# Transposes by pairs, spread tap tables, later stages and another slab order in a twelve-layer kernel

## The chip, the core and the metric

The kernel runs on one core of a Trainium2 chip. The core has a tensor engine (PE; its weight loads are listed apart as PEld), a vector engine (DVE), a scalar engine (ACT), GpSimd (POOL) and a queue engine (SP), which here only issues DMAs. The metric is the device time of one launch in microseconds, median of several runs, lower is better. A trace of one profiled execution tells where it went.

## What is computed

Fourteen sublayers act in turn on a residual x of 256 rows and 1024 columns in float32: a first block of four pairs (mixer, feed-forward) and a second block of two triples (feed-forward, mix, feed-forward). Each normalises x, multiplies it by weights that are read once from DRAM, and adds the result to x:

```python
def swiglu(h, w_gate_up, w_down):
    gate, up = jnp.split(h @ w_gate_up, 2, axis=-1)
    return (jax.nn.silu(gate) * up) @ w_down
...
def first_block(...):
    for i in range(DEPTH):               # 4: fourier, s5, attention, fourier
        h = rms_norm(x, norm_mix_g[i])
        ...
        x = x + mix.astype(x.dtype)
        h = rms_norm(x, norm_ffn_g[i])
        x = x + swiglu(h, ffn_w_gate_up[i], ffn_w_down[i]).astype(x.dtype)
```

The S5 mixer is, for 64 groups of 16 columns, a linear recurrence over the 256 positions in both directions, then a gate. The kernel cuts the positions into 32 chunks of 8: inside a chunk it convolves with tap tables, between chunks it scans. The dilated attention has three groups of 16 heads, whose results are weighted by the softmax of their log sums. A mix sublayer joins a state-space branch (decays from running sums of a step size over positions, 16 heads) and an attention branch over 64 keys chosen by an index score.

## The kernel before

**Weights.** All matrices come as 774 slabs of 128x1024 (512 KB), in the order in which they are used (the class W; `add_in` and `add_out` build the list, lines 246 to 255). SP loads a slab into one of four `raw` buffers (L156); ACT rounds it to `whi` (L168), DVE makes the rest `wlo` (L169). Every float32 product is three PE passes (L306, L307, L308: whi with hi, wlo with hi, whi with lo of the other side). A slab is 12 matmuls of 128x512.

**Order.** The program is written out in one go; each engine executes its own list in order. `slab_step` calls `S.tick()` twice in a slab, after six matmuls each. All other work is a task: `S.defer(fn, n)` puts it n ticks later, `S.pace(fns, every, wait)` puts several in a row, and `S.require(task)` forces a task, with those due earlier, where its result is needed. So the place of a transpose or a small product among the weight products is set by numbers of ticks.

**PSUM.** Four banks (`acc`) hold the sums of weight products, four (`aux`) everything else.

**Feed-forward** (`ffn`, eight of them). `in_proj` takes 11 blocks of four slabs. Each block's gate and up are evicted to `hb` (L467, L468); three ticks later a task of its own makes four transposes into one aux bank (L475) and `hT.put` splits them (L450, L451). `out_proj` takes 22 slabs: half 0, then half 1 of the 1024 output columns. At the end of a half x is updated (L433), and `half_ready` transposes it for the next layer (L380).

**S5.** Its tables are made during the first feed-forward by tasks on all engines, and kept in DRAM: wb (`s_wb`), ct (`s_ct`), and taps (`s_k`, written by POOL at L1572). In the S5 layer SP loads, in this order, wb, the four `local` tables (L1579: each 1 MB in eight pieces, 16 partitions of 16 runs of 128 numbers) and eight ct tables (L1541). PE makes the chunk ends (L1680, L817), then `part(k, 0)` for eight k with the local tables, and `part(k, 1)`, `part(k, 2)` with ct and the states H (L1758). DVE runs two scans, each of 30 steps of three operations (L1726, L1727, L1730): after the first ISC = 28 operations of scan 0 the two are interleaved, and ACT copies the states to H (L1740, L1741). While scan 1 goes on alone, DVE transposes the finished results (L1819). A task `rest` makes the last parts, k from 4 to 7, once scan 1 has ended.

**Attention.** `permuted_rstd` turns rsq of x to another order of rows by small products (L572), ahead of all blocks; it is needed from the second group of heads on. Then 18 blocks of four slabs make q, k and v; qk is evicted at L651 after transposes of qsq (L640). The heads are done in four units, each with four items (two head pairs by two row halves). `start_unit` runs the items as a pipeline, one item each AE = 4 ticks, with these stages and their ticks: scores 0 (PE L677), highest 1, exps 2, divide 4 (DVE, then POOL L696 on two tiles), probs 6 (PE L703), evict_probs 7 (ACT L711), values 10 (PE L723), put 11 (ACT L730, DVE L731). `oT.tasks` make the output product wait for put.

**Mix.** The first part of the state-space branch is paced on DVE and ACT, one step each SS = 3 ticks after STEPS = 6: decay, ratio, series, softplus, sums, keep, turn, spread. `spread` copies the running sums to `csT` (L1064), writes them to DRAM (L1066) and reads them back on all partitions as `csb` (L1069). Each head then needs ACT `seg` from csb (L1105), DVE (L1111), and PE (L1118 to L1120). The heads' place among the ticks is set by other joins, not by csb.

Of the kernel before, what the change touches and what calls it, by code (L numbers as in the profile page):

```python
# [17 lines left out]
P = 128  # L18
# [17 lines left out]
BB = 12  # L36
AR = 13
GD = 3
SS = 3
ISC = 28  # L40


DS = (0, 1, 2, 3, 4, 4, 5, 5)
# [11 lines left out]
ISM = 1000  # L55
EA = 11
UNITS = (None, 0, 1, 2, None, 3)
MIX_ORDER = tuple("qi bc x0 z0 x1 z1 q0 k0 v0 q1 k1 v1".split())


# [146 lines left out]
def tile_two_blocks(ctx: ExitStack, tc: tile.TileContext, A, out, upto=None, taps=None):  # L207
# [41 lines left out]
        for b, s in order_in(nblk):  # L249
            W.add(ap[base + b, s])  # L250

    def add_out(ap, nk):
        for h in range(2):
            for s in range(nk // 2):
                W.add(ap[h, s])

    layers = []
    for i in (range(6) if upto is None else upto):
        if i >= 4:
            i -= 4  # L260
            layers.append(("ffn1", i))
            add_in(A["ffn1_in"][i], 11)
            add_out(A["ffn1_out"][i], 22)
            layers.append(("mix", i))
            for b, s in order_in(12)[:8]:
                W.add(A["mix_in"][i, b, s])
            W.add(A["mix_small"][i])
            for b, s in order_in(12)[8:]:
                W.add(A["mix_in"][i, b, s])
            add_out(A["mix_out"][i], 16)  # L270
            layers.append(("ffn2", i))
            add_in(A["ffn2_in"][i], 11)
            add_out(A["ffn2_out"][i], 22)
            continue
        kind = i % 3
        if kind == 0:
            layers.append(("fourier", i))
            W.add(A["dft_d"])
            W.add(A["dft_t"])
            add_out(A["fnet_w_out"][i // 3], 8)  # L280
        elif kind == 2:
            layers.append(("attention", i))
            add_in(A["qkv"], 18)
            add_out(A["attn_o"], 8)
        else:
            layers.append(("s5", i))
            add_in(A["s5_glu"], 4)
        layers.append(("ffn", i))
        add_in(A["ffn_in"][i], 11)
        add_out(A["ffn_out"][i], 22)  # L290
# [131 lines left out]
                if b == 1 and after_head is not None:  # L422
                    after_head()

    def out_proj(src, nk, scale, xn):

        for h in range(2):
            ps = [acc() for _ in range(NT)]
            for s in range(nk // 2):
                slab_step(ps, src, 2 * s, W.take(), s == 0, s == nk // 2 - 1)  # L430
            for t in range(NT):
                xs = x[:, t, h * 512:(h + 1) * 512]
                nc.vector.scalar_tensor_tensor(xs, ps[t], scale, xs, OP.mult, OP.add)  # L433
            xn.half_ready(h)

    class Chunks:

# [20 lines left out]

    def ffn(xn, scale, nxt):
        hT = Chunks(22)  # L460

        def evict(b, ps):
            hb = tmp(name="hb")
            for t in range(NT):
# [2 lines left out]
                nc.scalar.activation(s, ps[t][:, :256], AF.Silu, scale=r)  # L467
                nc.vector.scalar_tensor_tensor(hb[:, t * 256:(t + 1) * 256], ps[t][:, 256:], r, s,  # L468
                                               OP.mult, OP.mult)

            def trans():
                pt = aux()
                for u in range(2):
                    for t in range(NT):
                        nc.tensor.transpose(pt[:, u * T + t * P:u * T + (t + 1) * P],  # L475
                                            hb[:, t * 256 + u * P:t * 256 + (u + 1) * P], ident)
                hT.put(2 * b, 2, pt)

            hT.tasks[2 * b] = hT.tasks[2 * b + 1] = S.defer(trans, 3)

        in_proj(xn, 11, evict)
        out_proj(hT, 22, scale, nxt)
# [73 lines left out]
    def attention(xn, nxt):  # L556
# [38 lines left out]
        def evict(b, ps):  # L595
            half, u, g = unit_block(b)
            if u is None:
                v = v_tile(half, g)
                for t in range(NT):
                    r = xn.rstd[:, t:t + 1] if g == 0 else rk[:, t:t + 1]  # L600
                    nc.scalar.activation(v[:, t], ps[t], AF.Copy, scale=r)
                if g == 2 and b // 3 % 3:
                    start_unit(UNITS[b // 3 - 1], 2)
                return
# [131 lines left out]

        def start_unit(u, wait):
            items = [(u, hp, t) for hp in range(2) for t in range(NT)]
            stages = ((put, 11), (values, 10), (evict_probs, 7), (probs, 6), (divide, 4), (exps, 2),
                      (highest, 1), (scores, 0))  # L740

            def step(n):
# [14 lines left out]
            return xn.chunk if u is not None or g == 0 else xn.chunk_by_parity  # L757

        S.require(xn.tasks[0])
        permuted_rstd()  # L760
        in_proj(xn, 18, evict, src)
        out_proj(oT, 8, 1.0, nxt)

    TWO_PI = (6.28125, 0.0019350051879882812, 2 * math.pi - 6.28125 - 0.0019350051879882812)
    ROUND = 1.5 * 2 ** 23
# [54 lines left out]
    def mixer(xn, nxt, li):  # L820
# [193 lines left out]
        def steps():  # L1014
# [55 lines left out]
                                                             ap=[[0, P], [1, 8 * T]]))  # L1070
                bc_ready()

            S.pace([decay, ratio, lambda: series((15, 13, 11, 9)), softplus, sums, keep, turn, spread], SS, STEPS)

        def similar():

# [199 lines left out]
    class S5:  # L1276
# [5 lines left out]
        def __init__(self):  # L1282
# [6 lines left out]
            self.wb_d = dram.tile([8, P, 2048], F32, name="s5_wb")  # L1289
            self.ct_d = dram.tile([8, P, 2048], F32, name="s5_ct")  # L1290
            self.kd = dram.tile([16, P, 240], F32, name="s5_k")
            self.wb, self.ct = {}, {}
            self.plan()

# [248 lines left out]
        def taps(self, m, ct):  # L1543
# [27 lines left out]
            if m % 2 == 1:  # L1571
                nc.gpsimd.dma_start(self.kd[m - 1:m + 1, :112].rearrange("m k x -> k m x"),  # L1572
                                    self.kt[:112, :480].rearrange("p (m x) -> p m x", m=2))

        def load_local(self, i):
            t = big(F32, "local")
            kd = self.kd.rearrange("m (q k) x -> k (m q) x", q=4)
            for j in range(8):
                nc.sync.dma_start(t[16 * j:16 * j + 16].rearrange("p (g x) -> p g x", g=16),  # L1579
                                  kd[:16, 16 * i:16 * i + 16, (7 - j) * 16:(7 - j) * 16 + 128])  # L1580
            return t

        def first_half(self, xn):
# [460 lines left out]
```

## Time and profile before

| | |
|---|---|
| time, median of 3 runs | 2555.62 us (2554.61 to 2557.14) |
| time of the profiled execution | 2555.06 us |
| its span | 2553.1 us |
| PE busy | 2460.1 us, 96% |
| DVE busy | 1615.5 us, 63% |
| ACT busy | 1331.1 us, 52% |
| POOL busy | 106.8 us, 4% |
| DRAM read, written | 437.57 MB, 16.50 MB |

Times in the trace count from the start of the span. The stretches that matter: the first feed-forward from 65 to 288.6 us, S5 from there to about 372, attention from 593.4 to 917.3, the two mix layers from 1523.4 to 1753.7 and from 2127.1 to 2357.4. In a timeline a row is a start, a duration, the engine, the line, the operation, and in brackets the idle time ahead of it with what ended it; rows of the same kind that follow each other are joined, with their count. Durations of matmuls overlap, so the cost of one is the distance of starts. A granted clock (PEclk) of 1.00 is 2.4 GHz, 0.50 is 1.2 GHz.

### The profile page before, as it was taken

The numbers are of one execution on the slowest core, as the hardware profiler recorded it, in microseconds if no ns is written. First come the engines' busy times: TensorE is split into PE (matmuls) and PEld (weight loads), VectorE is DVE, ScalarE is ACT, GpSimd is POOL, SyncE is SP. The second block draws the span as 40 slices with busy tenths as digits, with TensorE's granted clock in tenths as the row PEclk, the third lists the DMA queues.
The fourth block names the chain that finished last, engine by engine and source line by source line (L and its number), as shares of the span: only waits on it lengthen the run. The fifth ranks groups of instructions, "written<-read, shape, count | busy, mean of one in ns | idle before, by whom it ended". The sixth has DMA issues, their size and how long they took to land.

```text
span 2553.1 us, 34833 instructions
## 1 busy us (share of the span) xinstructions
PE 2460.1 (96%) x13048; PEld 2021.0 (79%) x13048; DVE 1615.5 (63%) x2847; ACT 1331.1 (52%) x2029; POOL 106.8 (4%) x127
## 2 busy tenths in 40 slices
PE   8999869999999999999999999999999999999998
PEld 7788558887777778888888888788888888788886
DVE  7988766554665655556555557776555555876554
ACT  5445555444555554444444446675444445775543
POOL 0111000000131410000000000000000000000000
PEclk9999979999999999999999999999999999999999
DMA  5777785665544546545555554545555555535554
GB/s 181 233 234 240 206 225 178 189 191 168 171 132 160 153 141 190 180 129 189 190 185 187 182 188 155 182 121 185 183 190 180 190 180 179 185 118 166 186 183 145
DMA packets 131850, 456.35 MB, mean 179 GB/s; under 512 B 14794, under 2 KB 23893, under 8 KB 129249
## 3 DMA queue, kind: packets, MB, share of 16 engines
q1 hardware_dynamic: 123616, 426.96, 52.8%
q0 software_dynamic: 7488, 26.51, 3.3%
q8 instruction: 103, 1.69, 0.3%
q10 hardware_dynamic: 576, 0.66, 0.1%
q14 instruction: 67, 0.54, 0.1%
HBM read 437.57 MB, written 16.50 MB: 178 GB/s over the span
## 4 chain that ended last, share of the span: by engine, by line
PE 41%; issue 29%; DVE 3%; ACT 2%; POOL 1%; DMA 1%; POOLq 0%; ACTq 0%; DVEq 0%
PE acc L306 12%; PE acc L308 12%; PE acc L307 12%; DVE wlo L169 1%; POOL sc L696 1%; PE aux L817 1%; ACT whi L168 1%; PE aux L475 1%; DMA csb<-cs_d 1%; PE aux L640 0%; PE aux L677 0%; PE aux L1213 0%; PE aux L703 0%; PE aux L723 0%; PE aux L380 0%
## 5 line engine op out<-in xcount | busy, mean ns | idle before, releaser
L169 DVE TENSOR_TENSOR wlo<-raw,whi 128x1024 fp32r<-128x1024 f32 (+1 forms) x774 | 922.2, 1219 | 371.7 <-ACT whi L168 370.0
L168 ACT ACTIVATE whi<-raw 128x1024 fp32r<-128x1024 f32 (+1 forms) x774 | 788.9, 1054 | 266.4 <-PE acc L308 245.3
L306 PE MATMUL acc<-whi,xhi 128*128 128x512 f32 (+1 forms) x2104 | 844.3, 401 | 2.1 <-DVE yflo L505 2.1
L307 PE MATMUL acc<-wlo,xhi 128*128 128x512 f32 (+1 forms) x2104 | 822.2, 391 | 3.2 <-DVE wlo L169 2.9
L308 PE MATMUL acc<-whi,xlo 128*128 128x512 f32 (+1 forms) x2104 | 823.6, 391 | 0.0
L308 PEld LDWEIGHTS acc<-whi,xlo 128*128 128x128 f32 x2104 | 398.2, 189 | 85.1
L306 PEld LDWEIGHTS acc<-whi,xhi 128*128 128x128 f32 x2104 | 399.3, 190 | 82.8 <-issue 3.8
L307 PEld LDWEIGHTS acc<-wlo,xhi 128*128 128x128 f32 x2104 | 399.6, 190 | 81.3 <-DVE wlo L169 4.9
L306 PE MATMUL acc<-whi,yhi 128*128 128x512 f32 x976 | 386.7, 396 | 1.0 <-ACT yhi L450 0.6
L307 PE MATMUL acc<-wlo,yhi 128*128 128x512 f32 x976 | 381.1, 391 | 3.1 <-DVE wlo L169 3.1
L308 PE MATMUL acc<-whi,ylo 128*128 128x512 f32 x976 | 381.4, 391 | 0.0
L467 ACT ACTIVATE silu<-acc,rsq 128x256 f32<-128x256 f32 x176 | 83.5, 475 | 288.8 <-PE acc L308 288.8
L468 DVE SCALAR_TENSOR_TENSOR hb<-acc,rsq,silu 128x256 f32<-128x256 f32 x176 | 84.4, 483 | 208.9 <-ACT silu L467 208.7
L307 PEld LDWEIGHTS acc<-wlo,yhi 128*128 128x128 f32 x976 | 183.8, 188 | 40.7 <-DVE wlo L169 3.9
L308 PEld LDWEIGHTS acc<-whi,ylo 128*128 128x128 f32 x976 | 183.6, 188 | 39.6 <-DVE ylo L451 0.7
L306 PEld LDWEIGHTS acc<-whi,yhi 128*128 128x128 f32 x976 | 183.7, 188 | 39.2 <-ACT yhi L450 1.0
L450 ACT ACTIVATE yhi<-aux 128x512 fp32r<-128x512 f32 (+1 forms) x104 | 58.6, 564 | 192.2 <-PE aux L475 189.7
L451 DVE TENSOR_TENSOR ylo<-aux,yhi 128x512 fp32r<-128x512 f32 (+1 forms) x104 | 67.5, 649 | 103.6 <-ACT yhi L450 103.6
L389 ACT ACTIVATE xhi<-aux,gains 128x256 fp32r<-128x256 f32 x104 | 40.8, 475 | 86.9 <-PE aux L380 86.9
L391 DVE SCALAR_TENSOR_TENSOR xlo<-aux,gains,xhi 128x256 fp32r<-128x256 f32 x104 | 43.1, 477 | 50.7 <-ACT xhi L389 50.7
L433 DVE SCALAR_TENSOR_TENSOR x<-acc,x 128x512 f32<-128x512 f32 x52 | 35.6, 690 | 56.5 <-PE acc L308 56.5
L696 POOL TENSOR_SCALAR sc<-sc,st 128x512 f32<-128x512 f32 x32 | 51.8, 1626 | 293.0 <-DVE st L694 278.7
(357 smaller groups left out, 1826.8 us busy)
## 6 DMA issues: line engine op xcount, KB each, us to landing
raw<-in_ffn_in_dram SPq DMA_DIRECT2D x352, 512.0 KB, 4.2
raw<-in_ffn_out_dram SPq DMA_DIRECT2D x176, 512.0 KB, 4.1
raw<-in_mix_in_dram SPq DMA_DIRECT2D x96, 512.0 KB, 3.6
raw<-in_qkv_dram SPq DMA_DIRECT2D x72, 512.0 KB, 3.7
raw<-in_mix_out_dram SPq DMA_DIRECT2D x32, 512.0 KB, 3.6
raw<-in_fnet_w_out_dram SPq DMA_DIRECT2D x16, 512.0 KB, 3.7
s_ct<-s5set POOLq DMA_DIRECT2D x16, 512.0 KB, 4.2
raw<-in_s_glu_dram SPq DMA_DIRECT2D x16, 512.0 KB, 4.5
```

Source lines behind the costliest of these rows:

```text
L168: self.nc.scalar.activation(hi[:, :w], r, AF.Copy)
L169: self.nc.vector.tensor_tensor(lo[:, :w], r, hi[:, :w].bitcast(F32), OP.subtract)
L306: nc.tensor.matmul(ps, lhs.hi, rhs.hi, start=start, stop=False, skip_group_check=True)
L307: nc.tensor.matmul(ps, lhs.hi, rhs.lo, start=False, stop=False, skip_group_check=True)
L308: nc.tensor.matmul(ps, lhs.lo, rhs.hi, start=False, stop=stop, skip_group_check=True)
L389: nc.scalar.activation(hi, p, AF.Copy, scale=g)
L391: nc.vector.scalar_tensor_tensor(lo, p, g, hi.bitcast(F32), OP.mult, OP.subtract)
L450: nc.scalar.activation(p.hi, ps, AF.Copy)
L451: nc.vector.tensor_tensor(p.lo, ps, p.hi.bitcast(F32), OP.subtract)
L467: nc.scalar.activation(s, ps[t][:, :256], AF.Silu, scale=r)
L468: nc.vector.scalar_tensor_tensor(hb[:, t * 256:(t + 1) * 256], ps[t][:, 256:], r, s, OP.mult, OP.mult)
L696: nc.gpsimd.tensor_scalar(s, s, st[:, 3:4], None, OP.mult)
```

## The change

Seven edits:

- The transposes of a feed-forward's blocks run by pairs (blocks 0 and 1, 2 and 3, and so on; block 10 alone), as one task three ticks after the second of the pair.
- The tap tables are spread to the order of use in DRAM. After every fourth call that makes taps, `spread_taps` is paced, one piece each two ticks, from eight ticks on: 32 copies from `s_k` to `s_local`, issued by SP during the first feed-forward. `load_local` becomes one plain load of 1 MB.
- ISC is 45.
- `permuted_rstd` becomes a task six ticks later, required where the first block needs it.
- In attention the lags of probs, evict_probs, values and put become 7, 8, 11 and 12.
- The eight slabs of attention's output product come in the order ATTN_OUT, of (half, slab): both halves have their sums open at once.
- The steps of the running sums have places of their own: 2, 4, 6, 8, 12, 14, 16, 18 ticks after STEPS.

```diff
-SS = 3
-ISC = 28
+ISC = 45
...
+ATTN_OUT = ((0, 0), (0, 1), (0, 2), (1, 0), (1, 1), (0, 3), (1, 2), (1, 3))
...
-    def out_proj(src, nk, scale, xn):
-
-        for h in range(2):
-            ps = [acc() for _ in range(NT)]
-            for s in range(nk // 2):
-                slab_step(ps, src, 2 * s, W.take(), s == 0, s == nk // 2 - 1)
-            for t in range(NT):
-                xs = x[:, t, h * 512:(h + 1) * 512]
-                nc.vector.scalar_tensor_tensor(xs, ps[t], scale, xs, OP.mult, OP.add)
-            xn.half_ready(h)
+    def out_proj(src, nk, scale, xn, order=None):
+
+        n, ps = nk // 2, {}
+        for h, s in order or [(h, s) for h in range(2) for s in range(n)]:
+            if s == 0:
+                ps[h] = [acc() for _ in range(NT)]
+            slab_step(ps[h], src, 2 * s, W.take(), s == 0, s == n - 1)
+            if s == n - 1:
+                for t in range(NT):
+                    xs = x[:, t, h * 512:(h + 1) * 512]
+                    nc.vector.scalar_tensor_tensor(xs, ps[h][t], scale, xs, OP.mult, OP.add)
+                xn.half_ready(h)
...
+        def trans(blocks):
+
+            pts = []
+            for b, hb in blocks:
+                pt = aux()
+                for u in range(2):
+                    for t in range(NT):
+                        nc.tensor.transpose(pt[:, u * T + t * P:u * T + (t + 1) * P],
+                                            hb[:, t * 256 + u * P:t * 256 + (u + 1) * P], ident)
+                pts.append((b, pt))
+            for b, pt in pts:
+                hT.put(2 * b, 2, pt)
...
-            hT.tasks[2 * b] = hT.tasks[2 * b + 1] = S.defer(trans, 3)
+            waiting.append((b, hb))
+            if b % 2 == 1 or b == 10:
+                blocks = waiting[:]
+                waiting.clear()
+                task = S.defer(lambda: trans(blocks), 3)
+                for c, _ in blocks:
+                    hT.tasks[2 * c] = hT.tasks[2 * c + 1] = task
...
+                if g:
+                    S.require(permuted)
...
-            stages = ((put, 11), (values, 10), (evict_probs, 7), (probs, 6), (divide, 4), (exps, 2),
+            stages = ((put, 12), (values, 11), (evict_probs, 8), (probs, 7), (divide, 4), (exps, 2),
                       (highest, 1), (scores, 0))
...
-        permuted_rstd()
+        permuted = S.defer(permuted_rstd, 6)
         in_proj(xn, 18, evict, src)
-        out_proj(oT, 8, 1.0, nxt)
+        out_proj(oT, 8, 1.0, nxt, ATTN_OUT)
...
-            S.pace([decay, ratio, lambda: series((15, 13, 11, 9)), softplus, sums, keep, turn, spread], SS, STEPS)
+            for fn, at in ((decay, 2), (ratio, 4), (lambda: series((15, 13, 11, 9)), 6), (softplus, 8), (sums, 12),
+                           (keep, 14), (turn, 16), (spread, 18)):
+                S.defer(fn, STEPS + at)
...
+            if m % 4 == 3:
+                S.pace([lambda j=j: self.spread_taps(m // 4, j) for j in range(8)], 2, 8)
+
+        def spread_taps(self, i, j):
+
+            kd = self.kd.rearrange("m (q k) x -> k (m q) x", q=4)
+            nc.sync.dma_start(self.local_d[i][16 * j:16 * j + 16].rearrange("k (g x) -> k g x", g=16),
+                              kd[:16, 16 * i:16 * i + 16, (7 - j) * 16:(7 - j) * 16 + 128])
 
         def load_local(self, i):
             t = big(F32, "local")
-            kd = self.kd.rearrange("m (q k) x -> k (m q) x", q=4)
-            for j in range(8):
-                nc.sync.dma_start(t[16 * j:16 * j + 16].rearrange("p (g x) -> p g x", g=16),
-                                  kd[:16, 16 * i:16 * i + 16, (7 - j) * 16:(7 - j) * 16 + 128])
+            nc.sync.dma_start(t, self.local_d[i])
             return t
```

On the queue of SP, in the S5 layer, the difference shows the 32 small loads of `local` giving way to four plain ones (the numbers of lines differ a little between the two kernels):

```order
-L1579 DMA local<-s_k 16x16x128 x32
-L1541 DMA ct<-s_ct 128x2048 x4
-L1541 DMA local<-s_ct 128x2048 x4
+L1602 DMA local<-s_local 128x2048 x4
+L1558 DMA ct<-s_ct 128x2048 x4
+L1558 DMA local<-s_ct 128x2048 x4
```

and ahead of it, in the first feed-forward, a copy now stands behind nearly every weight load from the 24th on, 32 in all.

On PE, at the first item of attention, the order before is (sc are the score tiles that POOL scales, qsq the rows of q or k of a later block):

```order
L308 MATMUL acc<-whi,xlo 128x512
L703 MATMUL aux<-ident,sc 128x128 x8
L640 MATMUL aux<-ident,qsq 128x128 x8
L306 MATMUL acc<-whi,xhi 128x512
```

and now:

```order
L654 MATMUL aux<-ident,qsq 128x128 x8
L305 MATMUL acc<-whi,xhi 128x512
L306 MATMUL acc<-wlo,xhi 128x512
L307 MATMUL acc<-whi,xlo 128x512
L305 MATMUL acc<-whi,xhi 128x512
L306 MATMUL acc<-wlo,xhi 128x512
L307 MATMUL acc<-whi,xlo 128x512
L717 MATMUL aux<-ident,sc 128x128 x8
```

The transposes of qsq and six weight matmuls now stand ahead of the transposes of probabilities.

On DVE, in the first mix layer, `csT` stood behind the last convolutions of the inputs, just ahead of the masks of bc (iscore and best belong to the index search):

```order
L979 SCALAR_TENSOR_TENSOR conv<-xbcT,conv 128x253 x2
L940 MAX best<-iscore 128x8 x2
L942 MATCH_REPLACE iscore<-best,iscore 128x128
L942 MATCH_REPLACE iscore<-best,iscore 128x256
L169 TENSOR_TENSOR wlo<-raw,whi 128x1024
L1064 COPY csT<-aux 16x256
L169 TENSOR_TENSOR wlo<-raw,whi 128x1024
```

and now stands ahead of them:

```order
L169 TENSOR_TENSOR wlo<-raw,whi 128x1024
L1078 COPY csT<-aux 16x256
L169 TENSOR_TENSOR wlo<-raw,whi 128x1024
L954 MAX best<-iscore 128x8 x2
L956 MATCH_REPLACE iscore<-best,iscore 128x128
L956 MATCH_REPLACE iscore<-best,iscore 128x256
L993 SCALAR_TENSOR_TENSOR conv<-xbcT,conv 128x255 x2
```

It moved past the last convolutions; on PE 129 rows lie between `turn` and the first head's products, where 98 did.

## Rows read from the trace of the kernel before

**Rows 1.** Waits of PE, whole span: line, releaser, us in total, times, longest.

```profile
PE acc L1758 <- DMA local<-s_k: 13.4, 3, 5.1
PE acc L1758 <- DMA ct<-s_ct: 8.0, 5, 5.1
PE aux L1118 <- DVE seg L1111: 7.6, 4, 3.6
PE aux L572 <- DVE rsq L322: 4.9, 1, 4.9
PE aux L640 <- ACT qk L651: 1.9, 2, 0.9
```

**Rows 2.** Stretches: length, busy time of each engine (count), PEclk, DMA share, GB/s.

```profile
124.00:190.00 66.00, 66.00 (x706) 52.59 (x705) 59.05 (x73) 30.30 (x52) 8.36 (x14) 1.00 0.74 241
...
318.00:344.00 26.00, 8.06 (x136) 6.39 (x140) 19.72 (x124) 16.46 (x20) 0.00 (x0) 0.50 1.15 192
...
600.00:604.00 4.00, 3.99 (x16) 3.31 (x17) 2.44 (x3) 0.00 (x0) 0.00 (x0) 0.50 0.27 45
...
1626.00:1632.00 6.00, 5.56 (x20) 5.03 (x21) 4.25 (x12) 4.92 (x10) 0.00 (x0) 0.50 0.56 187
```

**Rows 3.** Timeline of PE in a plain feed-forward, groups of eight and of four.

```profile
921.23 1.03 PE L380 MATMUL aux<-ident,x 128*128 128x128 f32 x8
922.02 0.48 PE L306 MATMUL acc<-whi,xhi 128*128 128x512 f32 x1
...
938.48 0.60 PE L475 MATMUL aux<-ident,hb 128*128 128x128 f32 x4
938.83 0.48 PE L306 MATMUL acc<-whi,xhi 128*128 128x512 f32 x1
939.14 0.39 PE L307 MATMUL acc<-wlo,xhi 128*128 128x512 f32 x1
```

**Rows 4.** Timeline of PE in S5, 314 to 368.

```profile
320.54 1.93 PE L1758 MATMUL acc<-local,U 128*32 128x128 f32 x32 [3.37 <-DMA local<-s_k]
...
341.48 1.94 PE L1758 MATMUL acc<-local,U 128*32 128x128 f32 x32 [5.14 <-DMA ct<-s_ct]
...
351.11 1.57 PE L1758 MATMUL acc<-ct,H 128*32 128x128 f32 x32 [0.65 <-DMA ct<-s_ct]
...
364.29 3.26 PE L1758 MATMUL acc<-local,H 128*32 128x128 f32 x112 [0.59 <-ACT H L1741]
```

**Rows 5.** Timeline of DVE in the S5 scans.

```profile
313.00 0.29 DVE L1726 TENSOR_TENSOR s5t<-s5a,es 128x128 f32<-128x128 f32 x1
...
313.84 0.29 DVE L1726 TENSOR_TENSOR s5t<-s5a,es 128x128 f32<-128x128 f32 x1
...
320.52 0.29 DVE L1726 TENSOR_TENSOR s5t<-s5a,es 128x128 f32<-128x128 f32 x1 [6.13 <-ACT es L1696]
...
321.00 0.28 DVE L1726 TENSOR_TENSOR s5t<-s5a,es 128x128 f32<-128x128 f32 x1
```

**Rows 6.** Attention: timeline of PE at the first item; ACT's evictions of probabilities by shape.

```profile
696.29 0.66 PE L703 MATMUL aux<-ident,sc 128*128 128x128 f32 x4 [1.57 <-POOL sc L696]
698.34 0.66 PE L703 MATMUL aux<-ident,sc 128*128 128x128 f32 x4 [1.39 <-POOL sc L696]
...
L711 ACT ACTIVATE pT<-aux 128x512 f32<-128x512 f32 x24 | 13.3, 603 | 3.7 <-PE aux L703 3.7
```

**Rows 7.** Waits of PE in 600 to 877, and in 877 to 904.

```profile
PE aux L703 <- POOL sc L696: 9.9, 10, 1.8
...
PE aux L703 <- POOL sc L696: 4.9, 4, 2.6
```

**Rows 8.** First mix layer, timelines of POOL and ACT; PE's wait in 2200 to 2240.

```profile
1613.97 1.08 POOL L1069 DMA_DIRECT2D csb<-cs_d  x2 [3.12 <-ACT xnat L1000]
...
1621.06 0.80 ACT L1105 ACTIVATE seg<-csb,cs 128x256 f32<-128x256 f32 x2 [3.35 <-DMA csb<-cs_d]
...
PE aux L1118 <- DVE seg L1111: 3.1, 1, 3.1
```

More of the change, by code (lines that the diff above doesn't have):

```diff
@@ L250, in add_in, with add_out @@
             W.add(ap[base + b, s])
-    def add_out(ap, nk):
-        for h in range(2):
-            for s in range(nk // 2):
-                W.add(ap[h, s])
+    def add_out(ap, nk, order=None):
+        for h, s in order or [(h, s) for h in range(2) for s in range(nk // 2)]:
+            W.add(ap[h, s])
     layers = []
@@ L283, in tile_two_blocks @@
             add_in(A["qkv"], 18)
-            add_out(A["attn_o"], 8)
+            add_out(A["attn_o"], 8, ATTN_OUT)
         else:
@@ L423, in in_proj @@
                     after_head()
-    def out_proj(src, nk, scale, xn):
-        for h in range(2):
-            ps = [acc() for _ in range(NT)]
-            for s in range(nk // 2):
-                slab_step(ps, src, 2 * s, W.take(), s == 0, s == nk // 2 - 1)
-            for t in range(NT):
-                xs = x[:, t, h * 512:(h + 1) * 512]
-                nc.vector.scalar_tensor_tensor(xs, ps[t], scale, xs, OP.mult, OP.add)
-            xn.half_ready(h)
+    def out_proj(src, nk, scale, xn, order=None):
[9 more added lines that the diff above has]
+                xn.half_ready(h)
     class Chunks:
@@ L460, in ffn @@
         hT = Chunks(22)
+        waiting = []
+        def trans(blocks):
[9 more added lines that the diff above has]
+                hT.put(2 * b, 2, pt)
         def evict(b, ps):
@@ L469, in evict @@
                                                OP.mult, OP.mult)
[L471 to L477, printed above, removed]
-            hT.tasks[2 * b] = hT.tasks[2 * b + 1] = S.defer(trans, 3)
+            waiting.append((b, hb))
[5 more added lines that the diff above has]
+                    hT.tasks[2 * c] = hT.tasks[2 * c + 1] = task
         in_proj(xn, 11, evict)
@@ L1291, in __init__ @@
             self.kd = dram.tile([16, P, 240], F32, name="s5_k")
+            self.local_d = dram.tile([4, P, 2048], F32, name="s5_local")
             self.wb, self.ct = {}, {}
```

## The prediction

> **What bounds the kernel now.** I began with the engines' shares: TensorE (PE) is busy 2460.1 of 2553.1 us, so only time in which PE waits, or runs at the lower of its two clocks, can be won. The waits of PE by line [rows 1] name the places, and they are few: the S5 convolution waiting for its tables (13.4 and 8.0 us), the first head product of each mix layer (7.6 in four, the longest 3.6), one wait of 4.9 for rsq at the start of attention, 1.9 for qk; and in attention the transposes of probabilities waiting for GpSimd, 9.9 and 4.9 us [rows 7]. Behind some of them PE's granted clock falls: the stretches [rows 2] show 0.50 (1.2 GHz, where 1.00 is 2.4) in 318 to 344, 600 to 604 and 1626 to 1632 us. At that level 6 us of matmuls hold 3 us of work. A plain feed-forward has no row among the waits. So I cost each edit at its own stall. Durations are of the execution of 2555.06 us; the median of the runs is 2555.62.
>
> **1. Transposes in pairs.** A group of four costs PE 0.35 us from its start to the next matmul's (938.48 to 938.83); a group of eight in another layer costs 0.79 (921.23 to 922.02) [rows 3]. Pairing makes 40 groups of eight and 8 of four out of 88 of four: 40 x (0.79 - 2 x 0.35) = +3.6 at most. The matmul behind either group is listed with 0.48, the next one with 0.39 [rows 3]; a pair pays that 0.09 once instead of twice: 40 x 0.09 = 3.6 back. The evictions stay the same in number, on engines with room. I take **0** (-0.5 to +3).
>
> **2. Tap tables.** Today 32 loads of 128 KB, in runs of 512 B, stand on the SP queue ahead of the ct tables. The first local product starts at 320.54, the fourth at 341.48 [rows 4]: three tables in 20.9 us, 7.0 for each MB, 0.87 for each load. The DMA engines are full meanwhile (share 1.15 at 192 GB/s in 318 to 344 [rows 2]). Afterwards four plain 1 MB loads stand there, like ct<-s_ct, whose four products follow the last local one within 9.6 us (341.48 to 351.11 [rows 4]), 2.4 for each MB. So all local products can be done by about 325, and the 21.4 us of waits go.
>
> What is late next is the scan on VectorE (DVE). Alone, three operations take 0.84 us (313.00 to 313.84), 0.28 each; two scans interleaved take 0.48 for three (320.52 to 321.00), 0.16 each [rows 5]. Of 90 operations of the first scan, 45 instead of 28 run alone: 17 more behind those that end near 314.4, to 319, still short of 320.52, when the second scan's input lets DVE go on (6.13 idle today, behind ACT es [rows 5]). Then 90 interleaved operations instead of 124, 14.3 us instead of 19.7, to 334.8 instead of 340.2. From there the second scan has 45 operations left instead of 28, 12.7 us alone, and between them sit two transposes of PE's results, which need H (2.4 us of copies on ScalarE, about 337) and two pairs of ct products (under 2 us each, to about 344). That puts the second scan's end near 357; ScalarE then copies H again. Today the last part of H releases PE at 364.29 [rows 4], after it I expect 359.5. So the waits of 21.4 shrink to a gain of 4.8; and PE, out of work for some 3 us before that, would run the 128 products (3.26 us for 112 [rows 4]) at the low clock, which takes back about half. **-2.5** (-5 to +1).
>
> The moved loads become 32 DRAM to DRAM copies, one per slab on SP, between weight loads in the first feed-forward. SP waits at them for GpSimd's table writes, due eight ticks before; behind it queue the raw loads, four slabs ahead of PE. No row shows such a copy. The nearest are today's loads at 0.87: 28 us of all DMA engines. The share is 0.74 in 124 to 190 [rows 2]; taken for the 53 of 66 slabs up to about 245, where the copies end, 0.26 x 121 = 31 us are free. Bounds: by the rate of the 1 MB loads (2.4 us per MB) 0.3 each, by 512 B pieces on both sides twice 0.87. I take 0.87, since pieces and bytes are those of today's loads, and **0** for PE; at 1.74 it is 56 us against 31 free and the four raw buffers' 10 of slack (four slabs of 12 matmuls at 0.23), so +15.
>
> The Trainium skill, "DMA: Bandwidth & Descriptors", section "Specifications", gives 512 B as the least transfer for line rate; here loads of just such pieces moved at 192 GB/s or less with the engines full, so the measurement decides. By the page a copy would take about 0.3 us (an estimate), and the slower rival below would have no ground.
>
> **3. Permuted scales six ticks later.** Today PE has eight transposes of x and then the small rsq products with nothing between, waits 4.9 for rsq [rows 1], and runs the next four us at clock 0.50, which loses 2 [rows 2]. In the new order 18 weight matmuls (4.1 us) stand ahead of the transposes and 18 behind them. The chain that makes rsq (x, xhi, squares, twelve DVE steps) hangs on ScalarE behind the transposes, so it starts 4.1 later while PE comes 8.2 later: 4.9 + 4.1 - 8.2 = 0.8 stays. The clock's 2 go, and about 1 for small gaps around the transposes, x among them (an estimate). **-7** (-8.4 to -5).
>
> **4. Attention lags.** Each item comes every four ticks; GpSimd scales its two score tiles, two ticks before PE transposes them. PE waits 1.57 for the first and 1.39 for the second, which it can start 2.05 apart [rows 6]. One tick more is six matmuls, 1.36 us, and 2.2 where the eight transposes of qsq fall into it, as the order shows. Of the 9.9 in the steady part [rows 7] two such pairs (6.2) keep 1 to 1.5 each, the single waits of 0.5 to 0.9 go; the two waits for qk (1.9) go with the longer cover. 11.8 - 2.8 = **-9** (-11.8 to -4). Against it: evict_probs and put now fall into the tick of the next scores, see the rivals.
>
> **5. Output order.** In the dense tail PE has almost no weight products from 877 to 903 and waits 4.9 for GpSimd, 2.6 of it first [rows 7]. The order of slabs puts two more (5.4 us) ahead of the last unit. The scores and highest of that unit are then covered, so about the 2.6 goes, less 0.4 for what moves: **-2.2** (-4.9 to +1). The next feed-forward's first transposes come two slabs later; three ticks are left, enough if nothing else slips.
>
> **6. Running sums.** csb is issued by GpSimd at 1613.97, its first half releases ScalarE's seg at 1621.06 after 3.35 idle, PE waits 3.6 behind that and 6 us at clock 0.50 cost 3 [rows 1, 2, 8]; the other mix layer waits 3.1 [rows 8], and its clock will do the like. csT stands some six ticks, 8.2 us, earlier on DVE, while the heads keep their place, so csb would land near 1613, before seg is due. 3.6 + 3.1 + 2 x 3 = 12.7; I keep 0.2 for wlo standing ahead of seg on DVE: **-12.5** (-13.5 to -8). If DVE, which makes softplus and the index search in one queue, is late, up to half of a layer's loss stays.
>
> Sum: 0 - 2.5 - 7 - 9 - 2.2 - 12.5 = -33.2, from 2555.1 to 2521.9; the median lies half a microsecond above the profiled execution, so **2522**.
>
> **The rivals.** (a) *Aux banks in attention.* evict_probs, put and scores share a tick; scores need banks that ScalarE frees, two evictions of 0.6 us each (128x512 [rows 6]). With 16 items at up to 1.2, 19 us would come against the 9 won: 2522 + 9 (half of them) to + 19, so about **2533**. For it: four banks only; against: ScalarE has half its time free and the weight products between cover a tick. (b) *csb or rsq is late again*, since DVE's queue is in order and the moved steps meet the index search there: half of terms 3 and 6 stays, +10, **2532**. The change then doesn't do what it says. (c) *Slower.* The copies fill the DMA engines and starve the weights. From 1.3 us each (31 + 10 over 32) PE stalls; at 2.3 the 33 us are lost; at 2.8, three times today's, it is **2571**. For it: a copy both reads and writes DRAM, and the share is already 0.74. Against: twice today's price is 1.74. (d) *S5 gains all*: only if the scan's tail were hidden, 4.8 at full clock and half of the 16.6 left: 2.3 + 8.3 more, **2511**.
>
> **How the numbers follow.** The forecast 0.63, (a) 0.13, (b) 0.11, (c) 0.07 (of this 0.02 ends within 0.2% and 0.04 beyond, the rest faster), (d) 0.06. The terms' own ends add to -44 and -12 (the copies' +15 aside), which do not fall together; 2510 to 2537 leaves out the far end of (a), most of (c), and little of (d). A measurement of this kernel can tell about 0.2% (5 us) from no change: faster 0.92, same 0.03, slower 0.05.
>
> **What would show it.** Right: no wait for csb or rsq above 1 us; the four local products between 309 and 325 and PE waiting for H instead; the waits for GpSimd near 3 steady and 2 in the tail; raw loads in the first feed-forward landing late without PE waiting for wlo there. Wrong: rows of PE waiting for a bank's eviction in attention (a), for seg with csb long landed (b), for wlo in 124 to 288 (c). Feed-forwards away from the first should keep their length within 0.5 us each.

## The result and the profile after

The changed kernel takes 2516.27 us (median of four runs, 2514.51 to 2516.88) beside 2555.11 for the kernel before in the same comparison; the ratio is 0.985 [0.983, 0.987], so 39 us less, where 33 were forecast. In the later comparisons the kernel before had medians of 2551.05 to 2553.70, by which it is 35 to 37. The profiled execution took 2516.76, its span is 2515.0.

Where it went, by the length of each layer (from the start of the last update of x of the one ahead to that of its own, in the two traces, so S5 counts with its output product up to 405 us; the terms are those of the prediction):

| layer | before | after | difference | terms |
|---|---|---|---|---|
| first feed-forward | 223.5 | 224.6 | +1.1 | copies: 0 |
| S5 | 116.6 | 113.6 | -3.0 | tables and ISC: -2.5 |
| attention | 324.0 | 300.5 | -23.5 | permuted -7, lags -9, order -2.2 |
| feed-forward behind it | 186.7 | 184.7 | -2.0 | order, pairs |
| each mix layer | 230.3, 230.2 | 225.8, 226.2 | -4.5, -4.0 | -6.25 each |
| each other feed-forward | 186.73 (behind S5 188.5, the last 185.8) | 186.36 (188.1, 185.6) | -0.37 (the last -0.2) | pairs: 0 |

Waits of PE in the trace after, whole span (line, releaser, us in total, times, longest):

```profile
PE acc L1780 <- ACT H L1763: 19.6, 3, 14.0
PE acc L306 <- DVE wlo L169: 9.5, 9, 2.4
PE aux L717 <- POOL sc L710: 6.1, 7, 1.8
...
PE aux L1134 <- DVE seg L1127: 1.2, 4, 0.4
...
PE aux L584 <- DVE rsq L321: 0.7, 1, 0.7
```

Against [rows 1] the waits for tables, for csb (through seg) and for qk are gone, that for rsq is 0.7 instead of 4.9, that for GpSimd 6.1 instead of 9.9 + 4.9 [rows 7]. Two have grown: PE now waits in S5 for H, the states of the scans, and 9.5 for wlo, 6.0 before.

S5, the timeline of PE after, then stretches (busy by engine, PEclk, DMA share, GB/s), to be held against [rows 4]:

```profile
318.25 4.74 PE L1780 MATMUL acc<-local,U 128*32 128x128 f32 x128
337.03 1.08 PE L1780 MATMUL acc<-ct,H 128*32 128x128 f32 x16 [14.04 <-ACT H L1763]
338.30 4.52 PE L1780 MATMUL acc<-ct,H 128*32 128x128 f32 x112 [0.18 <-ACT H L1763]
358.85 6.78 PE L1780 MATMUL acc<-local,H 128*32 128x128 f32 x128 [5.34 <-ACT H L1763]
...
350.00:358.00 8.00, 3.50 (x16) 2.57 (x14) 6.68 (x27) 3.90 (x5) 0.00 (x0) 1.00 0.00 1
358.00:364.00 6.00, 5.01 (x92) 4.24 (x96) 1.94 (x2) 3.35 (x6) 0.00 (x0) 0.50 0.05 11
```

All local products stand in one row, done by 323. H of scan 0 comes at 337.0 (337 forecast), the last parts start at 358.85 (359.5), behind 5.34 of idle and at clock 0.50: 6.78 us for 128 products, where before 112 took 3.26.

### The profile page after: what moved, and what is told of

Its sections match the earlier page's. It is cut to its first block, busy times and chain, and to the rows that moved or that the text cites. A ratio compares the mean times of both kernels' runs of the same rounds, so it can differ in the third digit from the quotient of the medians.

```text
span 2515.0 us, 34781 instructions
## 1 busy us (share of the span) xinstructions
PE 2444.7 (97%) x13048; PEld 2013.1 (80%) x13048; DVE 1616.4 (64%) x2847; ACT 1333.9 (53%) x2029; POOL 106.8 (4%) x127
## 4 chain that ended last, share of the span: by engine, by line
PE 88%; DVE 6%; ACT 3%; issue 1%; DMA 1%; POOL 0%; ACTq 0%; DVEq 0%; POOLq 0%
PE acc L305 26%; PE acc L306 26%; PE acc L307 26%; PE aux L471 2%; DVE wlo L169 1%; PE aux L831 1%; PE aux L379 1%; ACT whi L168 1%; DVE conv L993 1%; PE aux L691 1%; PE aux L737 1%; PE aux L717 0%; PE aux L1570 0%; PE aux L1229 0%; PE aux L654 0%
```

## The experiments

Each kernel is the changed one with the edit that is shown, if nothing else is said. Lengths of layers are compared, since a whole run moves by some microseconds: the kernel before took from 2544.5 to 2561.0 us. A length is that of one trace.

**Lags of attention back.**

```diff
-            stages = ((put, 12), (values, 11), (evict_probs, 8), (probs, 7), (divide, 4), (exps, 2),
+            stages = ((put, 11), (values, 10), (evict_probs, 7), (probs, 6), (divide, 4), (exps, 2),
```

> The changed kernel with attention's lags as they were (probs 6, evict_probs 7, values 10, put 11). Theory: GpSimd's two scaled tiles were late by up to 3 us for each item, and each such wait also pulled PE's clock to 1.2 GHz, so the lag alone carries the 17 us that the steady part won, not the 9 of the prediction: 2516 + 16 = about 2532, with waits for GpSimd near 10 us between the start of attention and the tail, and stretches of granted clock near 0.5 to 0.8 behind them. Rival 1 (the prediction's price: waits only, no clock): 2525, waits back, clock at 1.00. Rival 2: the steady part was won by the later permuted scales (blocks in another phase to the items), then 2516 to 2518 and no such waits.

2532.58 us; attention 318.0 instead of 300.5. Waits of PE, from 600 to the tail, and then a stretch of this kernel with the same stretch of the whole change:

```profile
PE aux L717 <- POOL sc L710: 10.7, 10, 1.8
PE aux L654 <- ACT qk L665: 1.9, 2, 0.9
...
743.00:755.00 12.00, 8.81 (x46) 7.23 (x46) 4.02 (x11) 7.22 (x14) 6.57 (x7) 0.86 0.54 154
...
733.00:745.00 12.00, 12.00 (x68) 9.65 (x67) 7.93 (x19) 7.68 (x16) 9.60 (x8) 1.00 0.70 195
```

The lag alone carries 17.5 us; both rivals fall. In the steady part the change won 17 us over the kernel before. The gaps of PE there are 11.8 us before and 0.9 after, which is 11 of them. Of the other 6, about 5 are matmuls at the lower clock, behind two pairs of such gaps; what the last one is stays open. In the kernel before the stretches around three pairs read:

```profile
717.00:732.00 15.00, 12.64 (x74) 9.85 (x69) 6.20 (x16) 7.46 (x15) 6.08 (x5) 0.89 0.26 85
752.00:764.00 12.00, 8.81 (x42) 7.01 (x40) 3.43 (x9) 7.11 (x14) 6.50 (x6) 0.72 0.53 153
777.00:792.00 15.00, 12.24 (x76) 9.64 (x75) 7.27 (x22) 8.70 (x16) 6.62 (x7) 1.00 0.30 85
```

In the second PE is busy for 8.81 of 12 us and has a mean clock of 0.72: by the clock column some 5 us of work are lost in the first two (0.11 x 15 + 0.28 x 12), and none in the third. So a pair of gaps may or may not bring the clock down: around the same three pairs it reads 1.00, 0.86 and 1.00 in the kernel with the old lags. The page's line of 40 slices rounds that away.

**Steps of the running sums back.**

```diff
-            for fn, at in ((decay, 2), (ratio, 4), (lambda: series((15, 13, 11, 9)), 6), (softplus, 8), (sums, 12),
-                           (keep, 14), (turn, 16), (spread, 18)):
+            for fn, at in ((decay, 3), (ratio, 6), (lambda: series((15, 13, 11, 9)), 9), (softplus, 12), (sums, 15),
+                           (keep, 18), (turn, 21), (spread, 24)):
```

> The changed kernel with the steps of the running sums three ticks apart again. Theory: csb is late again, PE waits 3.6 and 3.1 us for seg and runs behind that at 1.2 GHz for 6 us, but the two waits for wlo of 0.6 and 1.0 us in each mix layer, which the earlier steps brought on DVE, go: +8.5 us, about 2525. Rival: the waits for wlo come from the feed-forward's or the slabs' own order and stay; then +11.5, about 2528.

2519.00 us (2514.0 to 2523.2). Mix layers 225.4 and 230.2: only the second lost. The expectation of +8.5 missed, and the two layers of this one trace say why. ACT's first seg in each, then PE's wait, then the clock behind it:

```profile
1588.78 0.80 ACT L1121 ACTIVATE seg<-csb,cs 128x256 f32<-128x256 f32 x2 [1.08 <-DMA csb<-cs_d]
2190.06 0.80 ACT L1121 ACTIVATE seg<-csb,cs 128x256 f32<-128x256 f32 x2 [4.30 <-DMA csb<-cs_d]
...
1594.17 0.41 PE L1134 MATMUL aux<-xnat,seg 128*128 128x64 f32 x2 [1.35 <-DVE seg L1127]
2195.44 0.41 PE L1134 MATMUL aux<-xnat,seg 128*128 128x64 f32 x2 [4.56 <-DVE seg L1127]
...
1592.00:1598.00 6.00, 4.65 (x28) 3.82 (x27) 5.09 (x13) 5.94 (x12) 0.00 (x0) 1.00 0.79 280
2196.00:2202.00 6.00, 6.00 (x30) 5.38 (x29) 4.54 (x13) 4.80 (x10) 0.00 (x0) 0.73 0.47 170
```

The same transfer, csb's first half, took 4.8 us in the first layer (issued 1583.92, there at 1588.75) and 7.3 in the second (2182.70 to 2190.03). The share of the DMA engines was 0.82 and 0.88 meanwhile; what made the difference is not shown. With the old places of the steps PE waits 1.3 us in the one case and keeps its clock, and 4.6 in the other and loses it. In the change csb is there 10 us ahead of its use and neither matters. The waits for wlo do go with the old steps (none in these two layers).

**Tap tables back.** `load_local` makes its 32 small loads, `spread_taps` is gone, ISC stays 45.

```diff
-            if m % 4 == 3:
-                S.pace([lambda j=j: self.spread_taps(m // 4, j) for j in range(8)], 2, 8)
...
-            nc.sync.dma_start(t, self.local_d[i])
+            kd = self.kd.rearrange("m (q k) x -> k (m q) x", q=4)
+            for j in range(8):
+                nc.sync.dma_start(t[16 * j:16 * j + 16].rearrange("p (g x) -> p g x", g=16),
+                                  kd[:16, 16 * i:16 * i + 16, (7 - j) * 16:(7 - j) * 16 + 128])
```

> The changed kernel without the spread copies, with the 32 small loads in the S5 layer as before, ISC still 45. Theory: the first feed-forward gets back its 1.1 us (wlo waits by 230 us), the S5 layer waits for its tables as before; whether it takes the 3.0 us back is the scan's to say: H is ready near 359 either way only if PE's ct products are ready for DVE at 341 and 344, and with the tables late they are at 347 and 352, so the second scan stands behind the transposes of y until 353 and ends near 364: +3 in S5 plus some us of it for the longer rest of scan 1, -1.1 in the feed-forward; 2518 to 2522. Rival (DMA is the bound of S5): more than +10, 2526 and up.

2519.54 us (2515.37, 2516.20, 2522.88 and 2524.58; the trace is of the third). In the trace S5 takes 121.5 instead of 113.6, the first feed-forward 222.3 instead of 224.6. The last parts start at 365.02, again behind H and not behind a table. Behind them is DVE's wait for the first ct product, of this kernel and then of the change:

```profile
338.08 1.94 PE L1781 MATMUL acc<-local,U 128*32 128x128 f32 x32 [5.19 <-DMA local<-s_k]
349.04 1.93 PE L1781 MATMUL acc<-ct,H 128*32 128x128 f32 x32 [0.57 <-DMA ct<-s_ct]
365.02 6.46 PE L1781 MATMUL acc<-local,H 128*32 128x128 f32 x128 [4.54 <-ACT H L1764]
346.04 0.72 DVE L1842 STREAM_TRANSPOSE y<-acc 128x512 f32<-128x512 f32 x1 [11.79 <-PE acc L1781]
...
341.13 0.72 DVE L1841 STREAM_TRANSPOSE y<-acc 128x512 f32<-128x512 f32 x1 [5.34 <-PE acc L1780]
```

Late tables cost through the scan: DVE stands for the products that it must transpose, 11.8 us instead of 5.3, with 45 operations of scan 1 behind that. The rival of +10 falls. What the loads are worth is not settled: 7.9 us in S5 in this trace, where +3 and some had been expected, but two of the four runs were no slower than the change. With ISC 28 it is little: S5 takes 116.6 and 114.2 us in the two traces with the small loads (the kernel before, and the two parts alone, below), 114.8 in the one with the plain ones (below).

**Output order back.**

```diff
-            add_out(A["attn_o"], 8, ATTN_OUT)
+            add_out(A["attn_o"], 8)
...
-        out_proj(oT, 8, 1.0, nxt, ATTN_OUT)
+        out_proj(oT, 8, 1.0, nxt)
```

> The changed kernel with attention's output product in the old order of slabs. Theory: the waits for GpSimd in the tail hardly changed (4.9 before, about 5.2 after), so the order is worth the 1.3 us of the tail and the start of the next layer: 2517 to 2518.5. Rival (the prediction's price): +2.2 or more, with a first wait for GpSimd of 2.6 us again, 2518.5 to 2520. Second rival: with the new lags the old order leaves one tick less ahead of the last unit, and the tail is worse than in the kernel before, +4.

2515.43 us, which a run cannot tell from the change. Attention 300.5 as with the new order, the feed-forward behind it 186.36 instead of 184.71. So the order is worth 1.65 us, and not where the prediction had put it: the waits for GpSimd in the tail are 4.6 with the old order, 5.2 with the new one. What is won lies at the join to the next layer. This trace also has 1.5 us less in the Fourier layer behind that, which the edit doesn't touch; three other traces here have the same.

**Permuted scales and single transposes back**, in separate stages.

```diff
-            if b % 2 == 1 or b == 10:
+            if True:
...
         permuted = S.defer(permuted_rstd, 6)
+        S.require(permuted)
```

> The changed kernel with two parts undone in separate stages: the permuted scales at once, ahead of all blocks, and each block's transposes as a task of their own. Theory: at the start of attention PE waits 4.9 us for rsq again and runs 4 us at half clock: +7 in attention (300.5 to about 307). Each feed-forward after the first goes from 186.36 back to 186.73, +0.37, about +3 over eight. Rival for the pairs: the 0.37 comes from something else in the change (the matmul behind a group is what is saved, or nothing is): then the feed-forwards stay at 186.36. Together 2516 + 10 = 2526, or 2523.

2524.05 us. Attention 308.0 (+7.6), and the wait and the clock of the kernel before are back:

```profile
595.67 0.60 PE L584 MATMUL aux<-rsq,ident 128*64 128x1 f32 x8 [4.90 <-DVE rsq L321]
596.00:600.00 4.00, 4.00 (x15) 3.21 (x14) 2.44 (x3) 0.00 (x0) 0.00 (x0) 0.50 0.33 82
```

The feed-forwards are back at 186.73. The pairs are worth 0.37 us in each of six, 2.2 together; the first and the last differ by more than that between traces of the same code, so 3 for all eight is an estimate.

**ISC back at 28.**

```diff
-ISC = 45
+ISC = 28
```

> The changed kernel with ISC at 28 again, so with the plain table loads alone. Theory (the scans on DVE bound S5): the 17 operations less at the start leave DVE idle until 320.5 as in the kernel before, the first scan ends near 340, ct products near 346, and 28 operations are left: H ready about 2 us later than with 45, +1 to +3 in S5 (113.6 to about 115.5), 2518. Rival (ISC is what carries S5's 3 us, the loads give nothing): S5 back to 116.6, 2519. Second rival: with the tables early the split between the scans doesn't matter, since their sum of operations is the same: 113.6.

2516.99 us; S5 114.8, +1.2 beside the profiled execution of the change. Over the nine traces here whose S5 part is that of the change, S5 takes 111.6 to 114.1, 112.8 in the mean, so this is at the edge of what they can tell; the last parts begin at 362.20, 3.3 later, but at full clock (3.27 us for 112), with 0.56 us of idle ahead of them instead of 5.34.

**Each copy made twice**, the second time to a scratch tensor.

```diff
+            self.again_d = dram.tile([4, P, 2048], F32, name="s5_again")
...
+            nc.sync.dma_start(self.again_d[i][16 * j:16 * j + 16].rearrange("k (g x) -> k g x", g=16),
+                              kd[:16, 16 * i:16 * i + 16, (7 - j) * 16:(7 - j) * 16 + 128])
             nc.sync.dma_start(self.local_d[i][16 * j:16 * j + 16].rearrange("k (g x) -> k g x", g=16),
                               kd[:16, 16 * i:16 * i + 16, (7 - j) * 16:(7 - j) * 16 + 128])
```

> The changed kernel with each of the 32 copies made twice, the second time to a scratch tensor that nobody reads. The share of the DMA engines in 124 to 225 rose by 0.11 to 0.17 with the copies, which makes 0.46 us of all engines for each, not the 0.87 of the prediction. Theory by that: the share goes to about 1.0, and PE, with 10 us of slack in four raw buffers, waits little more: the first feed-forward 224.6 to about 225 to 226. Theory of the prediction (0.87 each): 56 us against 31 free, so +15, 2531. Rival: the 1.1 us that the first feed-forward lost are each copy's own delay of the raw load behind it (SP's queue in order), and double to +1.1.

2516.20 us; the first feed-forward takes 224.9 instead of 224.6. The stretch 150 to 175 in the kernel before, in the change, and here:

```profile
150.00:175.00 25.00, 25.00 (x271) 19.86 (x273) 22.16 (x28) 10.84 (x19) 3.55 (x6) 1.00 0.76 252
...
150.00:175.00 25.00, 25.00 (x280) 19.80 (x286) 22.10 (x28) 10.66 (x19) 3.06 (x6) 1.00 0.92 304
...
150.00:175.00 25.00, 25.00 (x264) 19.76 (x263) 22.10 (x29) 10.64 (x19) 3.25 (x6) 1.00 1.04 356
```

PE is busy throughout in all three. Over 124 to 225 the first set of copies adds 14.6 us of all DMA engines (the rises of the share times their stretches), 0.46 for each copy, the second 0.3. These are differences of two executions. The packets of 512 B in the trace tell it directly: from 119 to 226 us the kernel before has none, the change 8192, which took 15.0 us of all engines, and this kernel 16384, which took 30.8; that is 0.47 or 0.48 for each copy. The prediction's 0.87 was too dear, and the rival of starved weights far off.

**The second scan cut short.**

```diff
                 for c in range(1, 31):
+                    if w == 1 and c > 20:
+                        if c in (23, 30):
+                            yield lambda: states(w, c - 11 if c < 30 else 24, c + 1)
+                        continue
```

> The changed kernel without the last ten of the thirty steps of the second S5 scan (30 of its 90 operations are left out; the states are copied as they are). Theory (the scan's lone tail on DVE ends last): 30 x 0.28 = 8.4 us earlier, H ready near 351, before PE has ended its weight products near 354.5; so PE starts the last parts without idle and at full clock: 358.9 to 354.5, and 3.9 instead of 6.8 for the 128 products, -7 us in S5 (113.6 to about 106.5), 2509. Rival (tables or PE are what binds): nothing, 113.6.

2508.60 us; S5 106.8 (-6.8):

```profile
354.11 0.64 PE L1784 MATMUL acc<-local,H 128*32 128x128 f32 x16 [0.52 <-ACT H L1767]
355.34 3.26 PE L1784 MATMUL acc<-local,H 128*32 128x128 f32 x112 [0.58 <-ACT H L1767]
```

The last parts begin 4.7 earlier, without the idle, and at full clock (3.26 for 112). The lone tail of the scan on DVE is what ends last in the S5 layer of the change, as the prediction had it; table loads and PE are not.

**Two parts alone**, the lags and the steps of the running sums put into the kernel before.

```diff
-            stages = ((put, 11), (values, 10), (evict_probs, 7), (probs, 6), (divide, 4), (exps, 2),
+            stages = ((put, 12), (values, 11), (evict_probs, 8), (probs, 7), (divide, 4), (exps, 2),
...
-            S.pace([decay, ratio, lambda: series((15, 13, 11, 9)), softplus, sums, keep, turn, spread], SS, STEPS)
+            for fn, at in ((decay, 2), (ratio, 4), (lambda: series((15, 13, 11, 9)), 6), (softplus, 8), (sums, 12),
+                           (keep, 14), (turn, 16), (spread, 18)):
+                S.defer(fn, STEPS + at)
```

> The kernel before with only two parts of the change: the lags of attention and the earlier steps of the running sums. Theory (the parts are independent, each at its own stage): attention's steady part wins its 17 us as in the whole change (324.0 to about 307), and each mix layer goes to 225.8 to 226.2, with no wait for csb and 1.6 us of waits for wlo; nothing elsewhere; about 2555 - 17 - 8.5 = 2530. Rival (the lag pays only after the later permuted scales, or the tail takes it back): attention 315 and more. Rival for the mix layers: the waits for wlo come with the other parts; then 224.3 each.

2527.59 us (2527.45 to 2535.48). Attention 307.2 (-16.8), the mix layers 225.8 and 225.9, the feed-forwards 186.73. These two parts give the same without the others. Not expected: S5, whose code is that of the kernel before, takes 114.2 here and took 116.6 there.

**Steps in between.**

```diff
-            for fn, at in ((decay, 2), (ratio, 4), (lambda: series((15, 13, 11, 9)), 6), (softplus, 8), (sums, 12),
-                           (keep, 14), (turn, 16), (spread, 18)):
+            for fn, at in ((decay, 3), (ratio, 6), (lambda: series((15, 13, 11, 9)), 9), (softplus, 12), (sums, 14),
+                           (keep, 16), (turn, 17), (spread, 19)):
```

> The changed kernel with the steps at 3, 6, 9, 12, 14, 16, 17 and 19 ticks: the first four as in the kernel before, the last ones close together, csT one tick later than in the change. Theory: in the change csb lands 10 us ahead of its use, and the two waits for wlo come from softplus and its kin meeting the convolutions on DVE; with the first steps in their old places they go, and csb still lands some 5 us early: each mix layer 225.8 to about 224.3, 2513. Rival (the waits for wlo come from the index search and the convolutions moving against each other, whatever the steps' places): 225.8 still.

2517.59 us; each mix layer 226.95, 1.1 and 0.7 more than in the change. Waits of PE in the first mix layer, of this kernel and of the change:

```profile
PE acc L306 <- DVE wlo L169: 0.9, 1, 0.9
PE aux L1074 <- DVE cs L1069: 0.9, 1, 0.9
PE aux L1134 <- DVE seg L1127: 0.6, 2, 0.4
PE aux L1064 <- ACT whi L168: 0.3, 1, 0.3
...
PE acc L306 <- DVE wlo L169: 1.6, 2, 1.0
PE aux L1134 <- DVE seg L1127: 0.6, 2, 0.4
```

The first of the two waits for wlo went, as expected; the second stayed, as the rival had it, and the closer steps brought two new ones: `turn`, one tick behind `keep`, waits on PE for the copy of cs, which stands on DVE behind a wlo.

**The last unit's scaling on DVE.**

```diff
-                nc.gpsimd.tensor_scalar(s, s, st[:, 3:4], None, OP.mult)
+                (nc.vector if u == 3 else nc.gpsimd).tensor_scalar(s, s, st[:, 3:4], None, OP.mult)
```

> The changed kernel with the scaling of probabilities of attention's last unit on DVE instead of GpSimd (one engine name changed). In the tail PE still waits 5.2 us for GpSimd in six waits, its clock falls behind the first ones, and a load of bias stands in GpSimd's queue behind the scalings (DVE waits 5.8 for it). Theory: these waits go, with 1 to 2 us of low clock: -5 in attention (300.5 to about 295.5), 2511. Rival: the chain through scores, highest, exps, transposes and values is as long without GpSimd, and PE waits for DVE or ScalarE instead: -1 or nothing.

2508.64 us; attention 294.65 (-5.8). PE's clock stays at 1.00 from 848 to 872, and DVE's wait for bias is gone too. The scaling by engine (busy, mean ns), and all waits of PE in the tail:

```profile
L710 POOL TENSOR_SCALAR sc<-sc,st 128x512 f32<-128x512 f32 x24 | 39.5, 1652 | 249.0 <-DVE st L708 237.2 <-DVE rst L319 11.8
L710 DVE TENSOR_SCALAR sc<-sc,st 128x512 f32<-128x512 f32 x8 | 3.5, 482 | 0.0
...
PE aux L717 <- DVE sc L710: 0.7, 1, 0.7
PE acc L305 <- ACT yhi L744: 0.6, 2, 0.4
PE aux L737 <- ACT pT L725: 0.6, 2, 0.3
```

**Both together.**

> Both together, the scaling of the last unit on DVE and the steps at 3, 6, 9, 12, 14, 16, 17, 19. They lie in different stages, so their gains should add: 2516 - 5 - 3 = 2508, 1.8% below the kernel before and 0.3% below the change. Rival: one of the two gives nothing (2511 to 2513).

2510.38 us (five runs, 2509.18 to 2511.38); attention 294.6, mix layers 227.0. The steps in between cost some 1.1 us in each mix layer, as seen, so the expected 2508 was missed; the scaling on DVE alone is the fastest kernel here that does the whole work (two runs), at 0.983 [0.979, 0.988] of the kernel before.

## Why the prediction held, and where its terms were off

- **The method held:** the change works mostly at single places with a wait of PE in the trace before, and undoing the parts one by one, or putting two of them in alone, moves the layers they belong to. The direction, the range and the sign of each term came out. That the total came within 6 us is partly luck: the lags gave 8 us more than their term and the pairs 2 to 3 more, the running sums 4 less.
- **Lags (-9, measured -17).** The step that failed is the sum of waits without the clock. Of 11.8 us of gaps I kept 2.8; 0.9 stayed. And behind the waits I had read the clock in two stretches only (600 to 604, 1626 to 1632); behind two of the pairs of waits in attention it fell as well, and some 5 us went there. About 1 stays open. Lags back brought it all back.
- **Running sums (-12.5, measured -8.5).** The waits for seg went as forecast (7.6 to 1.2 us), and so did the clock's loss, which had been read in the first layer only. In the trace before, around the end of the wait in both:

```profile
1625.00:1633.00 8.00, 6.56 (x24) 5.86 (x25) 6.18 (x16) 6.37 (x13) 0.00 (x0) 0.57 0.54 186
2229.00:2237.00 8.00, 7.30 (x26) 6.43 (x27) 6.14 (x18) 5.66 (x11) 0.00 (x0) 0.57 0.45 139
```

  At 0.57 of the clock, 0.43 of the busy time is lost: 2.8 and 3.1 us, beside the 3 of the term. What failed is the step that moves csT earlier at no price to the rest of DVE's queue, but for 0.2: the earlier steps meet other work there, and wlo is late twice in each layer (1.6 and 1.8 us). That was rival (b)'s mechanism, priced at half the term, and it took a quarter; the 0.6 or so that is left of the miss stays open. Beyond that, the term depends on a transfer that takes from 4.8 to 7.3 us: with the old steps a layer takes 225.4 or 230.2. A price read from one profiled execution was one draw of it.
- **Permuted scales (-7, measured -7.2, and 7.6 when undone).** The weight matmul that starts 20.3 us behind the last update of x in the kernel before (at 613.67) starts 13.1 behind it in the change (604.14). 0.7 of the wait stayed, 0.8 had been worked out.
- **S5 (-2.5, measured -3.0 in one pair of traces).** All three steps held: the tables come early, the lone tail of the scan ends last, and nearly half the gain goes to the low clock. 21 us of waits were worth about 3. By the nine traces with the new S5 part (112.8 in the mean) and the two with the old one (116.6, 114.2) the gain is 2.6, and single pairs lie between nothing and 5. Cutting the scan showed the bound; rival (d) had no ground.
- **Copies (0, +15 as a bound).** The first feed-forward takes 223.3 to 224.6 in the ten traces with one set of copies and 222.3 to 224.0 in the three without: some tenths, and the 1.1 of the table is mostly the difference of two executions. My price of 0.87 each was nearly twice too high, and the copies were issued by 218.3, not up to 245. The price came from loads that write 128 numbers at a time to 16 partitions; a copy writes rows of 8 KB to DRAM. That this is the reason is not shown. The Trainium skill, "DMA: Bandwidth & Descriptors", section "Specifications", has line rate from 512 B on: the 0.3 us worked out from it, an estimate, was nearer to the 0.47 of a copy than the row that I preferred, while the loads of the kernel before, at 192 GB/s with the engines full, do not agree with it.
- **Output order (-2.2, measured -1.65).** The place was wrong. The waits for GpSimd in the tail stayed (5.2 us, where about 2 had been forecast), and the gain came at the next layer's start.
- **Pairs (0, measured -2.2 in six feed-forwards).** Below the term's end. In a plain feed-forward the transposes cost what was worked out (44 transposes take 0.41 us more, the matmuls behind the groups 0.4 less); the 0.37 is spread over the 760 other weight matmuls, 0.4 ns each. What does that stays open.
- **Rival (a)** has no row: no transposes or scores of the steady part wait for an eviction.

## What to carry to other kernels

Price a stall as its gap plus the matmuls behind it that run at the lower clock, and read the clock in a short stretch around each gap: a page in 40 slices hides it. Where a step waits for a DMA with little to spare, one trace shows one draw of the transfer's time; move the issue until the worst seen has room, and look then at what the moved steps delay on their engine. When a long wait is to go, work out what ends next: of 21 us in S5 the scan left 3.

## What the runs showed of the hardware

- The same broadcast load of 1 MB landed after 4.8 or 7.3 us in the two mix layers of one trace; one such wait of 1.3 us left PE's clock at 1.00, one of 4.6 brought it to 0.73 in the next six us.
- A copy of 128 KB in DRAM, from runs of 512 B to rows of 8 KB, took 0.47 us of all DMA engines by its packets; a load of the same runs to 16 partitions took 0.87 us with the engines full.
- Of two stretches with pairs of gaps of PE below 2 us, one of 12 us with 3.2 us idle had a mean clock of 0.72, one of 15 us with 2.8 us idle kept 1.00.
- Scaling 128x512 float32 numbers takes 1.65 us on GpSimd and 0.48 on DVE.
